# A decoder block on one core: GpSimd's subtractions moved behind VectorE's one-hots, expert weights issued ahead of row stores

## The chip, the cores and the metric

One core of a Trainium2 chip runs the whole kernel as one program. The metric is the time of one execution in microseconds on the device. Before the change three runs gave 703.48, 704.46 and 705.16 us, a median of 704.46.

## What is computed

One decoder block over 512 tokens of width 1024, in float32. Two branches (a chunkwise mLSTM and a differential attention) are merged by sigmoid gates and projected; then comes a routed feed-forward layer with 32 experts. The part that the change touches, cut from the reference:

```python
x = x + gate1 * (merged @ w_out[l])
h2 = rmsnorm(x, norm2_w[l]) * (1.0 + scale2) + shift2
x = x + gate2 * hierarchical_moe(h2, ...)

# hierarchical_moe
pg_top, g_idx = lax.top_k(softmax(hf @ w_rg + b_rg), 1)       # one of 4 groups
pe_top, j_idx = lax.top_k(softmax(e_sel), 2)                  # two of its 8 experts
weights = pg_top * pe_top / jnp.sum(pe_top, axis=-1, keepdims=True)
for e in range(32):
    act = jax.nn.silu(hf @ w_gate[e]) * (hf @ w_up[e])
    y = y + combine[:, e:e + 1] * (act @ w_down[e])
```

## The kernel before, in words

The kernel is written with an order of its own: each engine runs its instructions in the order of the program text, and waits only for data, for buffers and for its queue. The 512 tokens are four tiles of 128 rows, t = 0 to 3.

*The output projection.* `out_proj` multiplies the merged branches with `w_out` in 16 half steps. The first twelve serve all four tiles; the last four are done tile by tile (`x1_of(t)`), so that the rows of one tile are ready while TensorE works on the next. `x1_add` adds the residual on VectorE, in two halves of 512 columns, into the buffer `x1u[t]`. That buffer then holds the block's rows after the first residual.

*Routing of a tile.* `route_a(t)` (L1230) first issues the store of the rows to `out` on SyncE's queue, and then transposes them on TensorE. `route_s` takes the mean square on ScalarE and the power on GpSimd. `route_h` writes the high half of the normalized rows as float16 (`xnh`) on ScalarE. The low half `xnl` is what float16 leaves over. For tiles 0 and 1 VectorE computes it in one step (`route_l`); for tiles 2 and 3 `route_lg` (L1283) lets ScalarE scale `x1u[t]` in place and GpSimd subtract the high half, in two instructions of 512 columns each. `route_b` is the logits. `choices(a)` finds group and experts for the tiles a and a + 1, in some twenty small VectorE steps, each of which is a `yield`, so that other VectorE work can be put between them; for tiles 0 and 1 the two halves of `x1_add(3, ..)` stand after steps 0 and 4. `ranks(a)` counts with matmuls the place of each token at its expert.

*Gather.* `places_of(i, ts)` builds on VectorE the one-hots that send a token's row to its slot at the experts of pair i, two instructions for a pair and two tiles. `gather_mm` multiplies `xnh` and then `xnl` with these, so that the columns of 128 slots come out as a sum. For the first two pairs this is done in two parts, tiles 0 and 1 (`lo2`) and tiles 2 and 3 (`hi2`), so that the first can go on while the choices of the second are made. `idle` puts matmuls without use between them (the counts are `W1`). `evac` writes the gathered columns to `he`, four on ScalarE, four on VectorE. Between them stands `weights` (L1404): two small subtractions on GpSimd, two exponentials on ScalarE, four small VectorE steps.

*Experts.* 16 pairs of experts follow, each with a gate, an up and a down product, and an indirect DMA from GpSimd that adds the result's rows to `out`. That is why the rows have to be stored before.

*Weights.* Each expert has three matrices of 1 MB, 96 loads in all, in the order of use, all issued on SyncE's queue. `refill(n)` issues the next n of the list. The first 20 have buffers of their own: one in the room that the dense part leaves, 15 among the large units that also hold `w_out`, the merged branches (`mgh`, `mgl`) and `xnh`/`xnl`, two in the buffers of the split halves that the projection reads, two in a pool that opens behind the gather. After that a load takes the buffer of a matrix that has been used (`refill_used`). `REF` says how many are issued after which half step of the projection (12 in all), `RT[0]` how many before the tile-by-tile part, and `refill(R0 + R1)` in `out_proj` how many after the last tile's logits are prepared; the rest of the 20 follow in `experts`. SyncE works in program order, too: a load that waits for a buffer holds up the store behind it, and a store that waits for its rows holds up the loads.

*Around the change, in the order of the text:* `x1_of(3)`, `choices(0)` with the two additions of tile 3, `route_h(2)`, `route_a(3)`, `route_s(3)`, `route_b(2)`, `refill(3)`, `route_lg(2)`, `route_h(3)`, `route_lg(3)`; then `route_b(3, first_places)`, which puts `ranks(0)` and the one-hots of tiles 0 and 1 between its matmuls, `choices(2)`, GpSimd's products of one-hots (L1434), the first gathers, `ranks(2)`, the one-hots of tiles 2 and 3 with `weights` between them, and the second gather.

Of the kernel before, what the change touches and what calls it, by code (L numbers as in the profile page):

```python
# [15 lines left out]
AF = mybir.ActivationFunctionType  # L16
# [14 lines left out]
XS = 1024.0  # L31
NU = 18
BR = 5
R0, R1 = 3, 0
RT = (0, 0, 0, 0, 0)
REF = {4: 5, 7: 3, 11: 4}
W0 = (4, 3, 0, 2, 2, 1, 9)
EY, SY = 2, 0
W1 = (3, 2, 2)
GF = False  # L40
LP = lambda n: n % 2
GA = 2
# [15 lines left out]
def block_kernel(ctx, tc, x, c, positions, w_ada, b_ada, norm1_w, w_in, b_igate, b_fgate, conv_w, conv_b,  # L58
# [3 lines left out]
    PE, V, S, G, SP = nc.tensor, nc.vector, nc.scalar, nc.gpsimd, nc.sync  # L62
# [15 lines left out]
    def W2(name, shape, dt=F32):  # L78
        return wk.tile(shape, dt, name=name, tag="w2", bufs=7)
# [4 lines left out]
    def acc(name="acc"):  # L84
        return ps.tile([128, 512], F32, name=name, tag="acc", bufs=4)

    def pt(name="pt", shape=(128, 512), dt=F32):
        return ps.tile(list(shape), dt, name=name, tag="t", bufs=2)

    def ps2(name="ps2"):  # L90
        return ps.tile([128, 2, 512], F32, name=name, tag="s", bufs=1)
# [30 lines left out]
    def load_unit(us, c0, i, n=1024, src=None):  # L122
        kk = 2048 // n
        t = U("wp", [128, kk, n])
        src = win if src is None else src
        SP.dma_start(t, src[i * kk * 128:(i + 1) * kk * 128, c0:c0 + n].rearrange("(k p) f -> p k f", p=128))
        us.append(t)
# [931 lines left out]
    x1u = []  # L1059

    def load_x():

        st["y0"] = st["xw"].tile([128, 1024], F32, name="y0")
        for t in range(4):
            x1u.append(W5("xr", [128, 1024]) if t else st["y0"])
            SP.dma_start(x1u[t], x2[t * 128:(t + 1) * 128])
# [52 lines left out]
    def refill(n, q=SP):  # L1119
        for _ in range(n):  # L1120
            if loads:
                loads.popleft()(q)

    def expert_loads():
        ring.clear()
        loads.clear()
        n = 0
        for i in range(16):
            for w, src, j in (("g", wg_, 8), ("u", wu_, 8), ("d", wd_, 2)):
                for e in (eA[i], eB[i]):  # L1130
                    ld(n, (w, e), src[e], j)
                    n += 1

    ssq2 = const.tile([128, 4, 4], F32, name="ssq2")
# [6 lines left out]
    def nxt(n):  # L1141
        if len(sps) <= n < 16:

            w = wo[n // 4][:, (n // 2) % 2, (n % 2) * 512:(n % 2) * 512 + 512]
            V.tensor_mul(w, w, gbc[0][:, 0, (n % 2) * 512:(n % 2) * 512 + 512])
            sps.append(split(w))
# [4 lines left out]
    def out_proj():  # L1151
        dc.release()
        st["xw"] = ctx.enter_context(tc.tile_pool(name="morew", bufs=1, side="right"))
        routing_tiles()
        expert_loads()
        a_, b_, c_ = pt("oa"), pt("ob"), ps2("oc")
        banks = [a_, b_, c_[:, 0], c_[:, 1]] + [acc("od") for _ in range(4)]

        def mm(t, hh, k, wh, wl):
            ah, al = mgh[k // 4][:, k % 4], mgl[k // 4][:, k % 4]  # L1160
            sl = slice(t * 128, (t + 1) * 128)
            q = banks[2 * t + hh]
            PE.matmul(q, ah[:, sl], wh, start=(k == 0), stop=False)
            PE.matmul(q, ah[:, sl], wl, start=False, stop=False)
            PE.matmul(q, al[:, sl], wh, start=False, stop=(k == 7))

        for n in range(12):
            if n < 2:
                load_unit(wo, 0, n + 2, src=wout)
            if n == 2:  # L1170
                load_x()
            nxt(n + LA)
            for t in range(4):
                mm(t, n % 2, n // 2, *sps[n])
            refill(REF.get(n, 0))
            yield
        nxt(15)
        refill(RT[0])

        def x1_of(t):  # L1180
            for n in (12, 14, 13, 15):
                mm(t, n % 2, n // 2, *sps[n])

        def x1_add(t, *hs):
            for hh in hs or range(2):
                xa = x1u[t][:, hh * 512:(hh + 1) * 512]
                V.tensor_add(xa, banks[2 * t + hh], xa)

        x1_of(0)
        x1_add(0)  # L1190
        refill(RT[1])
        yield
        x1_of(1)
        x1_add(1)
        route_a(0)
        route_s(0)
        refill(RT[2])
        yield
        x1_of(2)
        x1_add(2)  # L1200
        route_a(1)
        route_s(1)
        route_h(0)
        route_b(0)
        refill(RT[3])
        yield

        route_a(2)
        route_l(0)
        route_h(1)  # L1210
        route_b(1)
        route_l(1)
        route_s(2)
        x1_of(3)
        routing_temps()
        for n, _ in enumerate(choices(0)):
            if n in (0, 4):
                x1_add(3, n // 4)
        route_h(2)
        route_a(3)  # L1220
        route_s(3)
        route_b(2)
        refill(R0 + R1)
        route_lg(2)
        route_h(3)
        route_lg(3)

    x1T = {}

    def route_a(t):  # L1230
        xa = x1u[t]
        SP.dma_start(ob[t // 2][:, t % 2], xa)
        h = x1T[t] = [W2("x1T", [128, 512]) for _ in range(2)]
        for hh in range(2):
            p = pt("x2p")
            for j in range(4):
                PE.transpose(p[:, j * 128:(j + 1) * 128], xa[:, (hh * 4 + j) * 128:(hh * 4 + j + 1) * 128], ident)
            if hh and t < 3:
                V.tensor_copy(h[hh], p)
            else:  # L1240
                S.activation(h[hh], p, AF.Copy)

    def route_s(t):
        xa = x1u[t]
        junk = W2("junk", [128, 1024], BF)
        S.activation(junk, xa, AF.Square, accum_out=ssq2[:, t, 0:1])
        G.tensor_scalar(ssq2[:, t, 1:2], ssq2[:, t, 0:1], 1.0 / 1024 / XS ** 2, EPS / XS ** 2, op0=ALU.mult, op1=ALU.add)
        rpow(ssq2[:, t, 2:3], ssq2[:, t, 1:2])

    def route_b(t, between=None):  # L1250
        h = x1T[t]
        p = acc("lgp") if t > 1 else ps2("lgp")[:, 0]
        for j in range(8):
            if j == 4 and between:
                between()
            PE.matmul(p[:, 0:36], h[j // 4][:, (j % 4) * 128:(j % 4 + 1) * 128], wr[:, j], start=(j == 0), stop=(j == 7))
        V.scalar_tensor_tensor(lg[:, t], p[:, 0:36], ssq2[:, t, 2:3], st["rbias"], op0=ALU.mult, op1=ALU.add)
# [8 lines left out]
    def route_h(t):  # L1266
        if t % 2 == 0:
            xn = U("xn", [128, 2, 2, 1024], F16)
            xnh.append(xn[:, 0])
            xnl.append(xn[:, 1])  # L1270
        S.activation(parts_of(t, xnh), rows_of(t), AF.Copy, scale=ssq2[:, t, 2:3])
# [7 lines left out]
    R = {}  # L1279
    flat = lambda ap: ap.rearrange("p t g j -> p t (g j)")  # L1280


    def route_lg(t):  # L1283
        S.activation(x1u[t], x1u[t], AF.Copy, scale=ssq2[:, t, 2:3])
        for a in range(2):
            G.tensor_sub(parts_of(t, xnl)[:, a], rows_of(t)[:, a], parts_of(t, xnh)[:, a])

    def routing_tiles():
        rp = ctx.enter_context(tc.tile_pool(name="routes", bufs=1, side="right"))
        for n, shape, dt in (("m12", [2, 4], F32), ("maskb", [4, 32], BF), ("pos", [4, 32], F32)):  # L1290
            R[n] = rp.tile([128] + shape, dt, name="r" + n)
        R["gm"], R["m1"], R["m2"] = ssq2[:, :, 3], R["m12"][:, 0], R["m12"][:, 1]

        wrf = wr.rearrange("p k f -> p (k f)")
        for c_ in range(2):
            R[f"ohf{c_}"] = wrf[:, c_ * 64:64 + c_ * 64].bitcast(BF).rearrange("p (t g j) -> p t g j", t=4, g=4)
# [55 lines left out]
    def dense():  # L1352
# [9 lines left out]
    oh = {0: W2("oh", [128, 4, 128], F16),  # L1362
          1: st["y0"][:, 512:768].bitcast(F16).rearrange("p (t f) -> p t f", t=4)}
# [3 lines left out]
    def places_of(i, ts=slice(0, 4)):  # L1367
        n = ts.stop - ts.start
        for h, e in enumerate((eA[i], eB[i])):
            V.tensor_tensor(oh[i if st.get("first") else 2][:, ts, h * 64:h * 64 + 64], sio2[:, h, None].to_broadcast([128, n, 64]),  # L1370
                            pos[:, ts, e:e + 1].to_broadcast([128, n, 64]), op=ALU.is_equal)
# [53 lines left out]
    def first_places():  # L1425
        ranks(0)
        places_of(0, lo2)
        places_of(1, lo2)

    route_b(3, first_places)  # L1430
    for _ in choices(2):
        pass
    for c_ in range(2):
        G.tensor_mul(ohf[c_], R["goh"][:, :, :, None].to_broadcast([128, 4, 4, 8]),  # L1434
                     R[f"oh{c_ + 1}"][:, :, None, :].to_broadcast([128, 4, 4, 8]))
    idle(W1[0], qq[1])
    gather_mm(0, pp, range(2), range(2), last=False)
    gather_mm(1, qq, range(2), range(2), last=False)
    wm = acc("warm")
    idle(W1[1], wm)  # L1440
    ranks(2)
    idle(W1[2], wm)
    places_of(0, hi2)
# [184 lines left out]
```

## Time and profile before

| | |
|---|---|
| timed runs | 703.48, 704.46, 705.16 us; median 704.46 |
| profiled execution | 705.96 us, span 704.2 us, mean granted TensorE clock 0.988 |
| TensorE matmul | 674.9 us busy, 96% of the span |
| TensorE weight load | 498.1 us, 71%, beside the matmuls |
| VectorE | 378.1 us, 54% |
| ScalarE | 234.3 us, 33% |
| GpSimd | 202.1 us, 29% |
| transfers | 171.50 MB, mean 244 GB/s; SyncE's queue 165.41 MB |

The profile is one execution; its spans and waits are times from the span's first instruction. The profiled execution's own time is 705.96 us, 1.8 us more than its span; a sum over rows is made against this execution, and the median of the timed runs is 1.50 us below it. A busy TensorE is one with a matmul in work, at whichever of its two clocks (1.2 or 2.4 GHz); the granted clock is 1.00 at the higher.

### The profile page before, as it was taken

To read this page: it belongs to the slowest core of one execution; us is meant where nothing else is said; L and a number is where in the kernel's file an instruction comes from. 1 tells how busy PE (TensorE), PEld (TensorE's weight loads), DVE (VectorE), ACT (ScalarE), POOL (GpSimd) and SP (SyncE) were. 2 spreads that over 40 slices of the span, in tenths; PEclk is the share of its full clock that TensorE was granted. 3 is DMA by queue.
4 is the path that set the end of the run, shared out by engine and by line. 5 is a ranking of instruction groups with operands and counts; after the bars stand their busy time and mean duration, and the time that the engine had idled before them with its cause. 6 is when DMAs were issued, how large, how long until landed. Compare 5 with 4: busy or idle time off the path is not lost. (4 is left out here: it accounts for less than half of the span.)

```text
span 704.2 us, 11486 instructions
## 1 busy us (share of the span) xinstructions
PE 674.9 (96%) x4478; PEld 498.1 (71%) x4478; DVE 378.1 (54%) x769; ACT 234.3 (33%) x513; POOL 202.1 (29%) x211
## 2 busy tenths in 40 slices
PE   6999999999998999999999999899999999999992
PEld 4678877878777777778886888676666666676650
DVE  3556669766685467773597764844322333223311
ACT  4446771452343355544322224441111111111100
POOL 5213253436552122333335431431111112111110
PEclk9999999999999999999999999999999999999998
DMA  9975069215125011045655894798999999999991
GB/s 307 354 228 199 1 257 406 100 55 179 52 75 180 1 60 61 1 180 181 252 180 190 337 423 186 283 403 326 382 382 375 407 397 389 386 373 382 408 380 24
DMA packets 47402, 171.50 MB, mean 244 GB/s; under 512 B 8025, under 2 KB 16354, under 8 KB 33006
## 3 DMA queue, kind: packets, MB, share of 16 engines
q1 hardware_dynamic: 44526, 165.41, 61.1%
q0 software_dynamic: 2752, 5.28, 3.8%
q8 instruction: 37, 0.61, 0.3%
q14 instruction: 23, 0.19, 0.1%
q10 hardware_dynamic: 64, 0.02, 0.0%
HBM read 164.37 MB, written 10.51 MB: 248 GB/s over the span
## 5 line engine op out<-in xcount | busy, mean ns | idle before, releaser
L443 POOL TENSOR_TENSOR hl<-wp,hl 128x512 fp32r<-128x512 f32 x60 | 84.8, 1415 | 172.8 <-ACT hl L442 157.3
L442 ACT ACTIVATE hl<-wp 128x512 fp32r<-128x512 f32 x120 | 74.5, 628 | 102.1 <-PE acc L500 44.9
L1559 PE MATMUL gu<-we,he 128*64 128x256 f32 x784 | 92.6, 379 | 0.0
L499 PE MATMUL acc<-hTh,hl 128*128 128x512 f32 x220 | 90.7, 412 | 0.1
L501 PE MATMUL acc<-hTh,hl 128*128 128x512 f32 x220 | 87.5, 398 | 0.0
L500 PE MATMUL acc<-hTl,hl 128*128 128x512 f32 x220 | 86.9, 395 | 0.0
L1559 PEld LDWEIGHTS gu<-we,he 128*64 128x64 f32 x784 | 59.7, 137 | 32.5 <-issue 6.8
L443 DVE TENSOR_TENSOR hl<-wp,hl 128x512 fp32r<-128x512 f32 x60 | 52.7, 879 | 51.5 <-ACT hl L442 51.4
L1383 PEld LDWEIGHTS <-xn 128*128 128x128 f16 x1024 | 61.6, 115 | 7.2 <-issue 5.4
L1563 ACT ACTIVATE sg<-gu 128x256 f32<-128x256 f32 x16 | 6.2, 385 | 170.7 <-PE gu L1559 170.7
L1383 PE MATMUL gp<-oh,xn 128*128 128x128 f16 x960 | 61.1, 224 | 0.5 <-DVE oh L1370 0.4
L1591 POOL DMA_INDIRECT out<-y,wr x11 | 19.3, 1756 | 140.2 <-DVE y L1586 116.2
L1564 DVE TENSOR_TENSOR sg<-sg,gu 128x256 f32<-128x256 f32 x16 | 6.8, 423 | 92.7 <-ACT sg L1563 92.7
L503 PE MATMUL acc<-hl,hTh 128*128 128x512 f32 x128 | 52.6, 411 | 0.0
L499 PEld LDWEIGHTS acc<-hTh,hl 128*128 128x128 f32 x220 | 41.8, 190 | 14.7 <-issue 4.7
L505 PE MATMUL acc<-hl,hTl 128*128 128x512 f32 x128 | 50.2, 392 | 0.0
L504 PE MATMUL acc<-hl,hTh 128*128 128x512 f32 x128 | 50.0, 391 | 0.0
L501 PEld LDWEIGHTS acc<-hTh,hl 128*128 128x128 f32 x220 | 41.6, 189 | 10.2
L1584 PE MATMUL o<-we,sg 128*64 128x512 f32 x192 | 47.4, 598 | 1.1 <-issue 1.1
L500 PEld LDWEIGHTS acc<-hTl,hl 128*128 128x128 f32 x220 | 41.9, 190 | 8.6
L868 DVE SCALAR_TENSOR_TENSOR wada<-wada,ccols 128x1024 f32<-128x1024 f32 x28 | 41.5, 1506 | 1.9 <-DMA wada<-in_w_ada 1.9
L1401 DVE TENSOR_SCALAR he<-gp,AB 128x128 f32<-128x128 f32 x64 | 21.9, 404 | 23.3 <-PE gp L1383 20.8
(364 smaller groups left out, 1174.5 us busy)
## 6 DMA issues: line engine op xcount, KB each, us to landing
we<-in_w_gate SPq DMA_DIRECT2D x25, 1024.0 KB
we<-in_w_up SPq DMA_DIRECT2D x24, 1024.0 KB
we<-in_w_down SPq DMA_DIRECT2D x24, 1024.0 KB
wp<-in_w_in SPq DMA_DIRECT2D x20, 1024.0 KB
wada<-in_w_ada SPq DMA_DIRECT2D x16, 1024.0 KB
ada<-in_w_ada SPq DMA_DIRECT2D x16, 512.0 KB
wx<-in_w_gate SPq DMA_DIRECT2D x6, 1024.0 KB
wp<-in_w_out SPq DMA_DIRECT2D x4, 1024.0 KB
```

The lines of the kernel that those rows point to most:

```text
L442: S.activation(hi, src, AF.Copy)
L443: (G if LP(n) else V).tensor_sub(lo, src, hi.bitcast(F32))
L499: PE.matmul(g.banks[b], wh[:, sl], ah, start=st, stop=False)
L500: PE.matmul(g.banks[b], wh[:, sl], al, start=False, stop=False)
L501: PE.matmul(g.banks[b], wl[:, sl], ah, start=False, stop=en)
L503: PE.matmul(g.banks[b], ah[:, sl], wh, start=st, stop=False)
L504: PE.matmul(g.banks[b], ah[:, sl], wl, start=False, stop=False)
L505: PE.matmul(g.banks[b], al[:, sl], wh, start=False, stop=en)
L868: V.scalar_tensor_tensor(t0[:, sl], cur[:, sl], ccol[:, j:j + 1], t0[:, sl], op0=ALU.mult, op1=ALU.add)
L1383: PE.matmul(ps_[c_][:, jj * 128:(jj + 1) * 128], parts_of(t, part)[:, c_, :, jj], o[:, t], start=first and part is xnh and jj == 0 and t = ...
L1559: PE.matmul(gu[r, k * 256:(k + 1) * 256], h[:, j, r], wt[key, e][:, j], start=(j == 0), stop=(j == 7), skip_group_check=True)
L1584: PE.matmul(o[r], aT[:, j, r], wt["d", e][:, j, n * 512:(n + 1) * 512], start=(j == 0), stop=(j == 1), skip_group_check=True)
```

## The change

Four things are changed. The scaling of tiles 2 and 3 by ScalarE stays where it was, in a function of its own (`route_ls`), while GpSimd's subtractions (`route_lg`) are issued in `first_places`, behind a copy of one element out of the last of VectorE's first one-hots, so that GpSimd starts them only when these are done. `refill` stands before `route_a(3)`, and so before the last tile's store, instead of behind `route_b(2)`, and issues four loads instead of three; two more loads are issued before the tile-by-tile part, ahead of all four stores. The second half of tile 3's addition follows step 2 of the choices instead of step 4. The unused matmuls between the gathers are 2, 4 and 2 instead of 3, 2 and 2.

```diff
-R0, R1 = 3, 0
-RT = (0, 0, 0, 0, 0)
+R0, R1 = 4, 0
+RT = (2, 0, 0, 0, 0)
-W1 = (3, 2, 2)
+W1 = (2, 4, 2)
         for n, _ in enumerate(choices(0)):
-            if n in (0, 4):
-                x1_add(3, n // 4)
+            if n in (0, 2):
+                x1_add(3, n // 2)
         route_h(2)
+        refill(R0 + R1)
         route_a(3)
         route_s(3)
         route_b(2)
-        refill(R0 + R1)
-        route_lg(2)
+        route_ls(2)
         route_h(3)
-        route_lg(3)
+        route_ls(3)

+    def route_ls(t):
+        S.activation(x1u[t], x1u[t], AF.Copy, scale=ssq2[:, t, 2:3])
+
     def route_lg(t):
-        S.activation(x1u[t], x1u[t], AF.Copy, scale=ssq2[:, t, 2:3])
         for a in range(2):
             G.tensor_sub(parts_of(t, xnl)[:, a], rows_of(t)[:, a], parts_of(t, xnh)[:, a])

     def first_places():
         ranks(0)
         places_of(0, lo2)
         places_of(1, lo2)
+
+        G.tensor_copy(R["ix"][0:1, 2:3], oh[1][0:1, 1, 127:128])
+        for t in (2, 3):
+            route_lg(t)
```

## Rows read from the trace of the kernel before

**Rows 1.** The page's part 1: busy us, share of the span, instructions.

```profile
PE 674.9 (96%) x4478; PEld 498.1 (71%) x4478; DVE 378.1 (54%) x769; ACT 234.3 (33%) x513; POOL 202.1 (29%) x211
```

**Rows 2.** Waits of PE, 425 to 704: total us, times, longest.

```profile
PE rkp L1348 <- DVE rmaskb L1338: 2.1, 1, 2.1
...
PE o L1584 <- issue: 1.1, 2, 0.6
...
PE gu L1559 <- ACT he L1399: 0.4, 1, 0.4
```

**Rows 3.** The same view of SyncE's queue, 380 to 704.

```profile
SPq L1112 <- PE gu L1559: 90.5, 30, 12.4
```

**Rows 4.** Timeline, 447 to 463: start, us, engine, line, operation, tiles, count.

```profile
447.81 4.63 POOL L1286 TENSOR_TENSOR xn<-xr,xn 128x512 f16<-128x512 f32 x4 [0.20 <-ACT xr L1284]
448.17 2.09 DVE L1370 TENSOR_TENSOR oh<-sio,rpos 128x128 f16<-128x128 bf16 x2
450.18 2.40 DVE L1370 TENSOR_TENSOR y<-sio,rpos 128x128 f16<-128x128 bf16 x2
452.51 0.24 DVE L1257 SCALAR_TENSOR_TENSOR lg<-lgp,ssq,rbias 128x36 f32<-128x36 f32 x1
452.77 1.95 PE L1383 MATMUL gp<-y,xn 128*128 128x128 f16 x32
457.86 0.49 DVE L1370 TENSOR_TENSOR oh<-sio,rpos 128x128 f16<-128x128 bf16 x2
458.40 3.47 PE L1383 MATMUL gp<-oh,xn 128*128 128x128 f16 x32 [0.40 <-DVE oh L1370]
461.91 1.51 ACT L1399 ACTIVATE he<-gp,AB 128x128 f32<-128x128 f32 x4 [4.17 <-PE gp L1383]
462.42 0.43 PE L1559 MATMUL gu<-wx,he 128*64 128x256 f32 x1 [0.44 <-ACT he L1399]
```

**Rows 5.** Windows near the end: us, engines' busy us, PEclk, DMA share, GB/s.

```profile
680.00:684.00 4.00, 4.00 (x40) 3.23 (x38) 0.75 (x1) 0.00 (x0) 1.54 (x1) 1.00 1.01 417
684.00:688.00 4.00, 3.07 (x30) 2.10 (x26) 0.42 (x1) 0.39 (x1) 0.00 (x0) 1.00 0.61 179
```

**Rows 6.** Timeline of ScalarE and GpSimd in the same stretch.

```profile
448.82 1.15 ACT L1284 ACTIVATE xr<-xr,ssq 128x1024 f32<-128x1024 f32 x1
456.75 0.41 POOL L1434 TENSOR_TENSOR wr<-rtmp 128x128 bf16<-128x128 f32 x1 [0.84 <-DVE rtmp L1319]
457.11 0.22 POOL L1406 TENSOR_TENSOR rtmp<-lg,ssq 128x16 f32<-128x16 f32 x1
457.53 0.21 ACT L1409 ACTIVATE rtmp<-rtmp 128x4 f32<-128x4 f32 x1
```

**Rows 7.** Timeline: SyncE's queue, its waiters, and the end of tile 3's projection.

```profile
378.50 0.38 SPq L126 DMA_DIRECT2D wp<-in_w_out  x1
379.34 0.34 SPq L900 DMA_DIRECT2D n<-in_norm_w  x1
384.61 0.26 POOL L901 TENSOR_SCALAR n<-n 128x8 f32<-128x8 f32 x1 [5.04 <-DMA n<-in_norm_w]
429.63 0.34 SPq L1232 DMA_DIRECT2D out<-y  x1
432.98 11.70 SPq L1232 DMA_DIRECT2D out<-xr  x3
442.96 0.40 PE L1165 MATMUL od<-hl,mgl 128*128 128x512 f32 x1
```

**Rows 8.** Windows around a store alone, and with loads queued.

```profile
430.00:432.00 2.00, 2.00 (x13) 1.66 (x12) 0.34 (x1) 0.00 (x0) 0.00 (x0) 1.00 0.66 262
447.00:460.00 13.00, 10.43 (x112) 8.51 (x112) 10.94 (x39) 3.31 (x5) 7.05 (x11) 0.81 0.99 406
```

**Rows 9.** Windows at TensorE's gap and behind it.

```profile
455.00:457.00 2.00, 0.19 (x3) 0.12 (x2) 1.69 (x10) 0.00 (x0) 0.66 (x2) 1.00 1.01 426
458.50:461.50 3.00, 3.00 (x31) 3.00 (x31) 0.92 (x5) 0.00 (x0) 2.00 (x6) 0.51 1.02 426
```

## The prediction, made before the changed kernel was run

> **What bounds the kernel now.** I read the engines' shares first, then TensorE's list of waits, then the timeline around the last stretch in which TensorE waits for anything, then SyncE's queue and the windows beside it. TensorE is busy for 96% of the span [rows 1]. From 425 us on it waits 2.1 us for the mask of the last two token tiles and 0.4 us for the first gathered columns, and for no weight transfer at all [rows 2]. SyncE, which issues the weights, is the one that waits, 90.5 us in 30 pieces, for TensorE to give buffers back [rows 3]. So from the first expert matmul at 462.42 [rows 4] to the end TensorE sets the pace. The transfers are only just in time: they are still running after 684 [rows 5], when the last pair's up projection has just begun, and the ring of buffers ties them to TensorE, so that if TensorE starts later or earlier they shift with it. The question is therefore what the change does to 462.42 and to the speed from there.
>
> What sets 462.42 is a chain [rows 4]: VectorE's logits of tile 3 at 452.51, its choices and ranks, the one-hots at 457.86, TensorE's gather of tiles 2 and 3 at 458.40, ScalarE's eviction at 461.91, the first expert matmul. In front of it stand four one-hots in 2.09 + 2.40 us beside GpSimd's four subtractions of 4.63 us; the same two one-hots at 457.86, with GpSimd out of the way, take 0.49.
>
> **The change part by part.**
>
> *GpSimd behind the one-hots.* Four one-hots at 0.49 us a pair are 0.98 instead of 4.49, so tile 3's logits come 3.4 us earlier at best, about 449.1. From logits to hi-tile one-hots it was 457.86 - 452.51 = 5.35. If the moved subtractions left the choices alone, the one-hots would start at 454.5. The four held-up one-hots took about one subtraction each (4.49 / 4 = 1.12 against 4.63 / 4 = 1.16), so as the other bound four of the choices' operations wait one subtraction each: 454.5 + 4 x 1.16 = 459.1, worse than before. Either way VectorE is not what is late next, as the following step shows. The small copy that holds GpSimd back is not in the trace; by the small GpSimd operations [rows 6] it is 0.2 to 0.4 us, if nothing hides it; here GpSimd has to wait for longer anyway (next step), so I count 0.
>
> The Trainium skill, "SBUF — State Buffer", section "Who interferes with whom", says that a VectorE instruction with two SBUF inputs is shut out by a GpSimd instruction that reads SBUF. By that rule the second bound above is the right one, and the gain on VectorE mostly moves from the one-hots to the choices; without the rule it would be 3.4 us. The rows on the one-hots [rows 4] fit it; no row of before has the long subtractions beside the choices. The sum would be the same by either, since the store decides it; by the rule, rival A would come out at its slow end, without it at its fast one.
>
> *The last store behind four loads.* This is the step that decides. The scaling of tile 3's rows by ScalarE is done in place, in the buffer that the store to `out` reads, so it can't start before that store has landed. Before, the store was issued at 444.3 (last of the three in the row from 432.98, which ends at 444.68) into an idle queue and the scaling started at 448.82 right behind ScalarE's own work [rows 6, 7]. Now `refill(4)` stands in front of it on the same queue. These loads take the buffers that tile 3's output projection has read last, so they can't go before 442.96 + 0.40 = 443.4 [rows 7]; the queue is idle then. How a transfer fares behind a load is in [rows 7]: the 4 KB of `n` were issued at 379.34, after a 1 MB load issued at 378.50, and GpSimd, waiting for them, began at 384.61, 5.3 us after their issue. So the queue is served in order. A store alone keeps the transfer engines busy for 0.66 x 2.0 = 1.3 us, and they begin 0.4 us or more after its issue at 429.63; four loads are 4.19 MB, at 406 GB/s 10.3 us [rows 8]. Sum: 443.4 + 0.7 + 10.3 + 1.3 + some 1.0 for a cold start and the landing = 456.7; I take 457, between 455.7 (nothing for start and landing) and 458 (twice that). Before, it was there before 448.8.
>
> From there the order of the engines' queues gives the first expert matmul, step by step [rows 4, 6]: scaling 1.14; two subtractions of tile 3, 2 x 1.16 = 2.3; behind them on GpSimd the two products of one-hots, 2 x 0.41 = 0.8; the two small subtractions and the exponentials on ScalarE, 457.11 to 457.74, 0.6; then ScalarE's eviction to the first matmul, 462.42 - 461.91 = 0.5 (the evictions are queued on ScalarE behind the exponentials, and these behind the scaling). Together 5.3, with six hand-overs of some 0.05 us 5.6: 457 + 5.6 = 462.6, against 462.42. TensorE's gather of the low halves needs the same subtractions and is done about 0.3 us before that. So the wait for the store takes back all that the one-hots gave: +0.2 us, between -1.1 and +1.2 with the bounds of the landing.
>
> *The clock.* What TensorE does in that time is little: it has gathered tiles 0 and 1 by about 454.5, fills in a few warm-up matmuls (W1 adds one in sum: 0.2 us, hidden in the same wait), gathers the high halves of tiles 2 and 3 in about 1 us and then stands until 462.6 but for some 1 us of low halves. Before, it had one such gap, nearly idle from 455.0 to 457.0, and the granted clock then fell to half (1.2 GHz): 0.51 from 458.5 to 461.5, so that the 32 gathers took 3.47 us, where 32 of them took 1.95 at full clock [rows 4, 9]. That low stretch lay on the gather. In the new order it falls on the first expert matmuls, which are limited by TensorE alone: each us at half clock loses half a us. A stretch like the one of before costs 3.47 - 1.95 = 1.5 us; with its edges 1.5 to 1.7, and a second one in a row is possible. The bounds are 0 and 3.2; I take 1.6.
>
> *Two loads ahead of all stores.* `RT[0] = 2` puts 2.10 MB, 5.2 us, ahead of the store issued at 429.63, for which the queue was empty [rows 7, 8]; the first store is later by at most these 5.2 us, the second and third by less, and nobody waits for them before ScalarE's scaling of tile 2, just ahead of that of tile 3 at 448.82. Cost 0. Their gain is that the weights run 5 us ahead; as TensorE waits for no weights [rows 2], this is worth 0 at the end. Without this cover it would be bounded by the same 5 us.
>
> *Row 3's second addition two steps sooner.* VectorE's steps are 0.2 us apart, so the last row is ready 0.2 us earlier, and its store behind the loads doesn't notice: 0, at best -0.2.
>
> Sum: +0.2 + 1.6 = +1.8 us. On the profiled execution, 705.96 us for a span of 704.2, this is 707.8. That execution was 1.5 us over the median of the timed runs, so the forecast for the median is 704.46 + 1.8 = 706.3.
>
> **The rivals.**
>
> *A: the store isn't late* (the loads wait for something longer, are overtaken, or ScalarE doesn't have to wait). Then the hi-tile one-hots set the time, at 454.5 to 459.1 by the two bounds above. The gather starts 0.5 later and takes 1.95 at full clock, since the gap is short, and 0.9 lie between its end and the first expert matmul (the gather's last result to the eviction, and 461.91 to 462.42): 457.9 to 462.4. It can't come before TensorE has done its first gathers and the four warm-ups either: 452.77 + 1.95 = 454.7 before, two more warm-ups 0.6, the ranks and one-hots 0.5 each [rows 4], and the same 1.95 + 0.9 give 459.2. So -3.2 to 0 us; I take the middle of the one-hots, 456.8, which gives 460.2: -2.2, 702.3. The landing decides: this holds when the store has landed by about 454, since 454 + 5.6 is 459.6. For it: two of the loads have a different kind of buffer (the split halves). Against it: the row of `n`, and 10 us of transfers that nothing shortens.
>
> *B: late, but the clock does not fall on the experts,* or the landing is at the low end: -1.1 to +1.2, I take +0.3: 704.8. For it: before, the low stretch was over when the gather was, and TensorE has some gathers in its gaps here, too. Against it: from about 458 to 462.6 it has 1 us of work, even less than in the gap of before.
>
> *C: more:* two low stretches in a row, or a landing at 458 with a whole one: +3.2 to +4.5, 708.3 on average.
>
> That the additional prefetch shortens the end is excluded by [rows 2, 3]: buffers come back only as TensorE uses them.
>
> **How the numbers follow.** About 0.2% (1.4 us) is what a measurement of this kernel tells from no change. Forecast 0.45 (705.4 to 707.4), B 0.26, A 0.17, C 0.12. Faster by over 0.2%: A less its upper edge, 0.15, and a little of B, 0.16. Within: the rest of A and B and the forecast's lower edge, 0.29. Slower: the rest, 0.55. The range from 702.2 to 708.9 leaves out about 0.08 below (half of A) and 0.06 above; as cases of both signs are in it, the forecast's own range is 705.4 to 707.4.
>
> **What would show it.** In the changed profile: the first four one-hots in about 1 us and tile 3's logits near 449.2; SyncE's last store issued at about 445.5, after four loads; ScalarE's scaling of tile 3 waiting for a transfer, and starting at 456 to 458; GpSimd's products of one-hots after 460; the first expert matmul at 462 to 463.5; granted clock 0.5 in a stretch after it. It is wrong if ScalarE's scaling starts before 453, or if TensorE's first expert matmul comes before 461 at full clock; and wrong in another way if TensorE later waits for weights.

## The result, and the profile after

The changed kernel takes 708.40 us, median of 6 runs (707.15 to 710.07); the kernel before took 704.42 beside it, median of 6 (703.34 to 705.35). The ratio is 1.0051, 95% interval 1.0032 to 1.0069: slower by half a per cent. The profiled execution is the slowest of the six, 710.07 us for a span of 708.4 (before: 705.96 and 704.2), so its span has grown by 4.1 us.

The timeline of the changed kernel around the gathers (start, us, engine, line, operation, tiles, count), answering [rows 4, 6]:

```profile
448.15 0.49 DVE L1372 TENSOR_TENSOR oh<-sio,rpos 128x128 f16<-128x128 bf16 x2
448.56 0.49 DVE L1372 TENSOR_TENSOR y<-sio,rpos 128x128 f16<-128x128 bf16 x2
...
449.33 2.25 POOL L1288 TENSOR_TENSOR xn<-xr,xn 128x512 f16<-128x512 f32 x2
...
449.63 0.26 DVE L1257 SCALAR_TENSOR_TENSOR lg<-lgp,ssq,rbias 128x36 f32<-128x36 f32 x1 [0.58 <-PE lgp L1256]
...
450.12 0.37 DVE L1315 TENSOR_TENSOR rtmp<-lg,ssq 128x8 f32<-128x8 f32 x1
...
450.53 1.09 DVE L1317 TENSOR_TENSOR rtmp<-rtmp,io 128x8 f32<-128x8 f32 x1
452.07 0.16 DVE L1319 TENSOR_REDUCE rtmp<-rtmp 128x2 f32<-128x8 f32 x1 [0.46 <-DVE rtmp L1317]
...
456.60 0.22 DVE L1352 SCALAR_TENSOR_TENSOR rpos<-rkp,rmaskb 128x64 f32<-128x64 f32 x1 [0.85 <-PE rkp L1350]
...
456.86 0.49 DVE L1372 TENSOR_TENSOR oh<-sio,rpos 128x128 f16<-128x128 bf16 x2
457.41 1.11 PE L1385 MATMUL gp<-oh,xn 128*128 128x128 f16 x17 [0.40 <-DVE oh L1372]
...
457.95 1.15 ACT L1284 ACTIVATE xr<-xr,ssq 128x1024 f32<-128x1024 f32 x1 [9.57 <-DMA out<-xr]
459.18 2.25 POOL L1288 TENSOR_TENSOR xn<-xr,xn 128x512 f16<-128x512 f32 x2 [7.60 <-ACT xr L1284]
...
460.38 2.04 PE L1385 MATMUL gp<-oh,xn 128*128 128x128 f16 x15 [1.87 <-POOL xn L1288]
461.40 0.77 POOL L1440 TENSOR_TENSOR wr<-rtmp 128x128 bf16<-128x128 f32 x2
...
462.12 0.22 POOL L1408 TENSOR_TENSOR rtmp<-lg,ssq 128x16 f32<-128x16 f32 x1
...
462.65 1.49 ACT L1401 ACTIVATE he<-gp,AB 128x128 f32<-128x128 f32 x4
...
463.15 0.69 PE L1565 MATMUL gu<-wx,he 128*64 128x256 f32 x1 [0.61 <-ACT he L1401]
```

VectorE's first four one-hots take 0.9 us instead of 4.5, and the hi-tile one-hots come 1.0 us earlier than in [rows 4]. But ScalarE's scaling of tile 3 waits 9.57 us until the store `out<-xr` has landed, and everything from 457.95 to the first expert matmul is the chain behind it. That matmul takes 0.69 us instead of 0.43: it runs at half clock, as the windows below show.

SyncE's queue, answering [rows 7]: four loads, and the last store behind them.

```profile
442.98 0.83 SPq L1112 DMA_DIRECT2D we<-in_w_up  x2
443.90 1.06 SPq L1112 DMA_DIRECT2D ws<-in_w_down  x2
445.08 0.39 SPq L1232 DMA_DIRECT2D out<-xr  x1
```

The trace's landing records put the loads at 447.9, 450.9, 453.4 and 456.7 and the store at 457.87, 12.8 us after its issue; the store before it, in an empty queue, was there 2.6 us after its issue (435.87 to 438.5). TensorE's waits from 425 us on (total, times, longest), answering [rows 2]:

```profile
PE gp L1385 <- POOL xn L1288: 1.9, 1, 1.9
...
PE gu L1565 <- ACT he L1401: 0.6, 1, 0.6
PE gu L1565 <- DMA wx<-in_w_up: 0.5, 1, 0.5
```

The first is new, and so is the last, a wait for weights in the last pair. Windows of the changed kernel (us, busy us of the engines, PEclk, DMA share, GB/s), answering [rows 5, 9]:

```profile
457.00:460.00 3.00, 1.11 (x18) 0.95 (x16) 0.35 (x2) 1.15 (x1) 0.82 (x1) 1.00 0.02 8
460.50:467.00 6.50, 5.82 (x37) 3.78 (x38) 4.03 (x16) 4.22 (x12) 5.06 (x12) 0.50 0.68 256
684.00:688.00 4.00, 3.52 (x32) 2.38 (x30) 0.00 (x0) 0.00 (x0) 1.46 (x1) 1.00 1.01 384
688.00:692.00 4.00, 3.07 (x28) 1.82 (x24) 0.42 (x1) 0.38 (x1) 0.00 (x0) 1.00 0.30 81
```

TensorE does 1.1 us of work in 3, then the granted clock is at its lower level (0.50, 1.2 GHz) for 6.5 us, most of it on experts. At the end the transfers run on until after 688.

One table carries most of what follows. All is counted from the end of the last matmul of tile 3's projection (443.36 in the kernel before, 442.79 + 0.40 in the changed one). That point is not the same in two profiles, even of kernels with the same code up to there: 442.57 in one run below and 445.63 in another. The first four columns are starts behind it; the fifth is from the first to the second pair's first matmul, the sixth from the last pair's first matmul to the end of its last product.

| kernel | scaling, tile 3 | logits, tile 3 | hi one-hots | first expert | pair 1 | last pair | timed ratio |
|---|---|---|---|---|---|---|---|
| before | 5.46 | 9.15 | 14.50 | 19.06 | 16.66 | 12.77 | 1 |
| changed | 14.77 | 6.45 | 13.67 | 19.96 | 18.63 | 14.33 | 1.0051 |
| e1 store first | 5.24 | 6.08 | 14.54 | 19.18 | 16.65 | 12.77 | 1.0000 |
| e2 own buffer | 5.11 | 6.44 | 14.53 | 17.62 | 16.64 | 13.11 | 1.0000 |
| e3 loads only | 14.51 | 7.22 | 12.39 | 19.70 | 19.42 | 12.77 | 1.0053 |
| e4 subtractions only | 5.24 | 6.44 | 14.54 | 17.58 | 16.65 | 13.76 | 1.0000 |
| e5 TensorE kept busy | 14.96 | 6.44 | 14.06 | 20.15 | 16.65 | 13.98 | 1.0029 |
| e6 store from ScalarE | 10.94 | 6.39 | 14.09 | 17.54 | 16.65 | 12.77 | 1.0009 |
| e7 low half on VectorE | - | 7.00 | 14.09 | 17.18 | 16.65 | 12.76 | 0.9989 |
| e8 the same, loads as before | - | 7.01 | 13.87 | 16.96 | 16.65 | 14.24 | 0.9987 |
| e9 e7 without filling | - | 7.01 | 12.34 | 15.43 | 16.65 | 12.75 | 0.9974 |
| e10 e9, filling earlier | - | 7.15 | 12.48 | 15.57 | 16.65 | 12.77 | 0.9975 |
| e11 e8 without filling | - | 7.00 | 12.35 | 15.44 | 16.65 | 12.76 | 0.9959 |

So the 4.1 us are: +0.90 to the first expert matmul, +1.97 in the first pair, +1.56 in the last, less some 0.15 before the projection's end and as much behind the last product.

### The profile page after: what moved, and what is told of

It reads as the page before. It is cut to its first block, busy times and chain, and to the rows that moved or that the text cites. A ratio compares the mean times of both kernels' runs of the same rounds, so it can differ in the third digit from the quotient of the medians.

```text
span 708.4 us, 11491 instructions
## 1 busy us (share of the span) xinstructions
PE 678.1 (96%) x4479; PEld 499.7 (71%) x4479; DVE 376.4 (53%) x769; ACT 234.0 (33%) x513; POOL 202.1 (29%) x212
## 3 DMA queue, kind: packets, MB, share of 16 engines
q0 software_dynamic: 2752, 5.28, 3.8%
## 5 line engine op out<-in xcount | busy, mean ns | idle before, releaser
L1565 PE MATMUL gu<-we,he 128*64 128x256 f32 x784 | 94.5, 382 | 0.0
```

The lines of the kernel that those rows point to most:

```text
L1565: PE.matmul(gu[r, k * 256:(k + 1) * 256], h[:, j, r], wt[key, e][:, j], start=(j == 0), stop=(j == 7), skip_group_check=True)
```

## The experiments

Theory: the store behind four loads makes the scaling late, and the lull that follows puts half clock on the experts. Rivals: the moved subtractions do the harm, by holding up the choices; or the weights' order does.

**The store alone, two ways.** e1 puts the loads behind the store again; e2 leaves the order and writes tile 3's scaled rows into tile 1's buffer, so that ScalarE need not wait.

```diff
-        refill(R0 + R1)
         route_a(3)
+        refill(R0 + R1)
```

> The changed kernel with one line moved: the four loads are issued behind the last tile's store instead of ahead of it; all else is as changed. Theory (the late store): ScalarE's scaling of tile 3 starts at about 448.4 with no wait, GpSimd ends its four subtractions at about 454, the first expert matmul comes at 459.5 to 462.4 instead of 463.15, with no half-clock stretch on the experts, and the time is 702.0 to 704.8 us where the kernel before has 704.4. Rival (the moved subtractions and the new counts of warm-up matmuls cost the time, the late store only coincides): the time stays at 707 to 709.

```diff
-        S.activation(x1u[t], x1u[t], AF.Copy, scale=ssq2[:, t, 2:3])
+        S.activation(x1u[1 if t == 3 else t], x1u[t], AF.Copy, scale=ssq2[:, t, 2:3])
...
-            G.tensor_sub(parts_of(t, xnl)[:, a], rows_of(t)[:, a], parts_of(t, xnh)[:, a])
+            G.tensor_sub(parts_of(t, xnl)[:, a], rows_of(1 if t == 3 else t)[:, a], parts_of(t, xnh)[:, a])
```

> The changed kernel, loads still ahead of the last store, but tile 3's scaled rows go into the buffer of tile 1, whose store has long landed, so that nobody waits for the last store. Theory (the wait for the store): as with the store first, 702.0 to 704.8 us, though the store itself lands at 457.9 as in the changed kernel. Rival (the four loads themselves cost the time, by what they take from the transfers or by late weights): 707 to 709, as changed.

Measured: 704.92 us, ratio 1.0000 [0.9986, 1.0014], and 704.63, 1.0000 [0.9984, 1.0015]. Either way the loss is gone, and no gain is left (e1's time is 0.1 us above the range expected, with before at 705.08 beside it). The timeline of e1:

```profile
443.09 0.33 SPq L1232 DMA_DIRECT2D out<-xr  x1
...
443.51 1.21 SPq L1112 DMA_DIRECT2D we<-in_w_up  x2
...
447.57 1.15 ACT L1284 ACTIVATE xr<-xr,ssq 128x1024 f32<-128x1024 f32 x1
...
448.45 4.50 POOL L1288 TENSOR_TENSOR xn<-xr,xn 128x512 f16<-128x512 f32 x4
...
456.87 0.49 DVE L1372 TENSOR_TENSOR oh<-sio,rpos 128x128 f16<-128x128 bf16 x2
...
457.42 3.55 PE L1385 MATMUL gp<-oh,xn 128*128 128x128 f16 x32 [0.40 <-DVE oh L1372]
```

The scaling doesn't wait, and all four subtractions now lie beside the choices: the one-hots at 456.87 are 14.54 behind the projection, as before (14.50). The gather takes 3.55 us, again at half clock, as in [rows 4].

**Each half of the change alone.** e3 is the kernel before with the loads moved; e4 is the changed kernel with the loads as before.

```diff
-R0, R1 = 3, 0
-RT = (0, 0, 0, 0, 0)
+R0, R1 = 4, 0
+RT = (2, 0, 0, 0, 0)
...
+        refill(R0 + R1)
         route_a(3)
         route_s(3)
         route_b(2)
-        refill(R0 + R1)
```

> The kernel before with the loads' part of the change alone: two ahead of the stores, four ahead of the last store; GpSimd's subtractions, the warm-up matmuls and the additions as before. Theory: ScalarE waits for the last store until about 458, the first expert matmul comes at 463 to 464 with a half-clock stretch behind it, 707 to 709 us: the whole loss comes with this part. Rival (the loss needs the moved subtractions): 703.5 to 705.5, as before.

e4 is the same diff the other way, on the changed kernel.

> The changed kernel with the loads as before (three, behind the last store, none ahead of the others): the moved subtractions, the new warm-up counts and the earlier addition alone. Theory: no wait for a store; the choices of tiles 2 and 3 are held up by the four subtractions instead of the one-hots, so the hi-tile one-hots come at 456.5 to 458.5 (457.86 before) and the time is 702.5 to 705.0 us. Rival (the moved subtractions lose): 706.5 or more. If the clear gain that the one-hots promise by themselves (3.4 us) were kept: under 702.

Measured: e3 709.02 us, 1.0053 [1.0032, 1.0074], the whole loss; e4 705.15, 1.0000 [0.9985, 1.0016], no loss, 0.15 us above its expected range. In e3 ScalarE's waits from 440 to 470 have the store as in the changed kernel:

```profile
ACT xr L1284 <- DMA out<-xr: 9.1, 1, 9.1
```

There VectorE is even 2.1 us ahead at the hi one-hots (12.39 against 14.50), since two of the subtractions wait for the scaling too and leave it alone; it is of no use. A window of e3 over the first experts:

```profile
462.30:469.00 6.70, 5.74 (x33) 3.27 (x32) 5.67 (x20) 4.22 (x12) 4.97 (x14) 0.50 0.84 315
```

The granted clock is 0.50, and pair 1 lasts 2.76 us longer. VectorE's timeline in e4 has what the moved subtractions cost:

```profile
451.13 0.37 DVE L1315 TENSOR_TENSOR rtmp<-lg,ssq 128x8 f32<-128x8 f32 x1
451.54 1.08 DVE L1317 TENSOR_TENSOR rtmp<-rtmp,io 128x8 f32<-128x8 f32 x1
453.08 0.16 DVE L1319 TENSOR_REDUCE rtmp<-rtmp 128x2 f32<-128x8 f32 x1 [0.46 <-DVE rtmp L1317]
453.27 0.47 DVE L1321 TENSOR_TENSOR rtmp<-io,rtmp 128x8 f32<-128x8 f32 x1
453.78 1.14 DVE L1330 TENSOR_TENSOR rtmp<-lg,rtmp 128x64 f32<-128x64 f32 x1
```

With no subtraction beside them, operations of these lines on tiles of 8 or 16 columns take 0.17 us (further on in e4), and the one on 64 columns 0.22 (in the first choices). The excess is 0.20 + 0.91 + 0.46 + 0.30 + 0.92 = 2.8 us, and the logits had come 9.15 - 6.44 = 2.7 us earlier. The two cancel: 14.54 against 14.50.

**The clock.** e5 is the changed kernel with unused matmuls in the lull, 12 ahead of the second gather instead of 2 and four behind it.

```diff
-W1 = (2, 4, 2)
+W1 = (2, 4, 12)
...
     gather_mm(0, pp, range(2), range(2, 4), first=False)
+    idle(4, wm)
```

> The changed kernel with matmuls without use in the time in which TensorE waits for the late low halves: 12 instead of 2 ahead of the gather of tiles 2 and 3, and four behind it. The first expert matmul should come at about 463.1 as in the changed kernel. Theory (the clock is the second term of the loss): no half-clock stretch on the experts, the second pair begins at about 479.8 instead of 481.8, and the time is some 2 us under the changed kernel's: 705.5 to 707.5. Rival (the first pair is slow for another reason, late weights or its own evictions): second pair at 481 or later, 707.5 to 709.

Measured: 707.16 us, 1.0029 [1.0017, 1.0042], 1.2 us below the changed kernel's 708.40 (which was timed beside other runs of before; by the ratios, 0.0022 x 705 = 1.6). The two intervals overlap, so the times by themselves leave the gain unsure; the windows show what changed:

```profile
457.00:461.00 4.00, 4.00 (x36) 2.31 (x35) 0.72 (x3) 1.15 (x1) 0.77 (x1) 1.00 0.18 71
461.00:467.00 6.00, 5.33 (x56) 3.55 (x55) 3.01 (x13) 3.55 (x11) 4.64 (x12) 1.00 0.61 206
```

The clock stays at its higher level and pair 1 takes 16.65 instead of 18.63, though the store is as late as ever. So the late start and the slow first pair are two costs, one from the store and one from the lull: TensorE's little work between 457 and 460.

**Another queue.** e6 issues tile 3's store from ScalarE.

```diff
-        SP.dma_start(ob[t // 2][:, t % 2], xa)
+        (S if t == 3 else SP).dma_start(ob[t // 2][:, t % 2], xa)
```

> The changed kernel with the last tile's store issued on ScalarE's queue instead of SyncE's, where the four loads stand ahead of it. Theory (it is the order within one queue that delays the store): it lands by about 450, ScalarE's scaling of tile 3 starts by 450.5, and the time is as with the store first, 703.5 to 706 us. Rival (the transfer engines are full and serve in order of issue whatever the queue): it lands near 457 and the time stays at 707 to 709.

Measured: 705.30 us, 1.0009 [0.9997, 1.0021]; most of the loss is gone, and nothing is gained. Timeline of ScalarE:

```profile
442.51 0.38 ACTq L1232 DMA_DIRECT2D out<-xr  x1
...
452.69 1.16 ACT L1284 ACTIVATE xr<-xr,ssq 128x1024 f32<-128x1024 f32 x1 [5.48 <-DMA out<-xr]
```

The store is issued 0.8 us behind the projection instead of 1.9, but it still takes 10.1 us beside them (it lands at 452.61, between the second load at 450.64 and the third at 454.31). So the landing came out as neither case expected: not by 450 and not near 457. It is early enough here, as the scaling is then no longer last. The profiled execution (702.77) is this kernel's fastest of 12, so its columns in the table flatter it.

**A version that gains.** The two halves of the change point to one thing: tile 3's subtraction should be beside nothing and wait for nothing. In e7 VectorE makes tile 3's low half itself (`route_l`, scaling and subtraction in one, out of the unscaled rows), behind the hi one-hots; GpSimd does tile 2 alone, and no later than before. e8 is the same with the loads as before.

```diff
         route_ls(2)
+        route_lg(2)
         route_h(3)
-        route_ls(3)
...
-        G.tensor_copy(R["ix"][0:1, 2:3], oh[1][0:1, 1, 127:128])
-        for t in (2, 3):
-            route_lg(t)
...
     places_of(0, hi2)
+    route_l(3)
     weights()
```

> The changed kernel with the low halves divided: GpSimd subtracts tile 2 at once, as before the change, and VectorE makes tile 3's low half in one step behind the hi-tile one-hots (as tiles 0 and 1 have it), so that no engine waits for the last store and GpSimd is never beside the choices. Expected from what was seen: two of the four first one-hots held up (lg of tile 3 near 451), hi-tile one-hots near 456.5, 1.5 us of VectorE behind them, first expert matmul at 459.8 to 461.0, 702.0 to 704.0 us. Against it: weights that come too late at the end (705), or the half-clock stretch on the gather or the experts (704 to 706).

> The same with the loads as before the change (three, behind the last store). If the weights that run ahead are worth nothing, as the prediction had it: the same time as with them, within 0.7 us. If they are worth something once TensorE is earlier: 1 to 2 us slower, with a wait for weights in the last pairs.

Measured: 703.63 us, 0.9989 [0.9976, 1.0003], and 704.28, 0.9987 [0.9976, 0.9999]: both a little below before, by less than 0.2%, and e7's interval still holds 1. VectorE's timeline in e7 says what is last now:

```profile
456.85 0.23 DVE L1352 SCALAR_TENSOR_TENSOR rpos<-rkp,rmaskb 128x64 f32<-128x64 f32 x1 [2.13 <-PE rkp L1350]
```

VectorE waits 2.13 us for TensorE's ranks, which are queued behind the first gathers, most of them at half clock, and four unused matmuls of 1.03 us together. e9 and e11 take the unused matmuls out of e7 and e8, and e10 puts eight of them in front of the logits of tiles 2 and 3 in e9.

```diff
-W1 = (2, 4, 2)
+W1 = (2, 0, 0)
```

> The kernel with tile 3's low half on VectorE (loads and store order as in the change), and the unused matmuls between the first gathers and the second taken out (W1 = (2, 0, 0) instead of (2, 4, 2)). In its parent TensorE ran the first gathers at half clock until 455.1, then four unused matmuls (1.03 us) and only then the ranks of tiles 2 and 3, for which VectorE waited 2.1 us. If this filling is on the path, ranks, one-hots and the first expert matmul come 0.9 to 1.2 us earlier (first expert matmul about 16.1 us behind the last matmul of tile 3's projection, instead of 17.18), and the time is 0.5 to 1.2 us below the parent's 703.63. The rival: without the filling the granted clock falls to half again on the second gather or the first experts, which costs 1.5 to 2 us; then the time is the parent's or up to 1 us above.

> As the run without the filling, and four unused matmuls of 512 columns put in front of the logits of tile 2 and of tile 3 each, where TensorE otherwise has transposes and 36-column products, after which its clock fell to half at 4.5 us behind the projection. If the fall follows from what TensorE does there, the half-clock stretch of 6.8 us starts later or is gone, the first gathers take 4 us instead of 6, and the first expert matmul comes up to 1.5 us earlier than without the early filling; time 701.5 to 703. The rival: eight matmuls cost 8 x 0.22 = 1.8 us in front of tile 3's logits and move ranks and one-hots back by as much, with the clock falling all the same: 0.5 to 1.8 us slower than without.

> As the run without the filling, with the loads as in the kernel before (no two ahead, three behind tile 2's logits). If the weights' stream bounds an earlier start (the last pair waited 1 to 1.5 us for its weights in the two profiles in which the experts began 1.5 to 2.9 us earlier with the loads as before), this one gains nothing over its own parent's 704.28, and the run with the loads ahead is 0.6 to 1.5 us faster. If the prefetch is worth nothing, the two are within 0.4 us.

Measured: e9 702.45 us, 0.9974 [0.9961, 0.9988]; e10 703.41, 0.9975 [0.9959, 0.9991]; e11 702.20, 0.9959 [0.9945, 0.9974]. From e8 to e11 the intervals are apart: the filling was on the path. From e7 to e9 they overlap, and the 1.75 us that the first expert matmul is earlier in e9's profile are more than the four matmuls; the last section comes back to this. In e11:

```profile
457.73 0.23 DVE L1352 SCALAR_TENSOR_TENSOR rpos<-rkp,rmaskb 128x64 f32<-128x64 f32 x1 [0.37 <-PE rkp L1350]
457.99 0.49 DVE L1372 TENSOR_TENSOR oh<-sio,rpos 128x128 f16<-128x128 bf16 x2
```

The wait is 0.37 us and the first expert matmul comes 15.4 us behind the projection, 3.6 earlier than before, with pair 1 at full clock. e10's profile shows no stretch at half clock around the gathers at all, yet it gains nothing over e9 (703.41 us is 0.4 above its expected range): the gathers are then faster than VectorE's choices, which TensorE waits for (1.2 us for `rmaskb`). And the loads ahead gain nothing either: e9 and e11 agree within their intervals, so the case that the prefetch would be worth 0.6 to 1.5 us in this pair fell. e11 is 0.4% faster than the kernel before and 0.9% faster than the changed one. Most of the 0.4% came with taking out the filling (0.9987 to 0.9959); that was not tried on the kernel before, so how much of it needs the low half on VectorE is not shown.

## Why the prediction was right or wrong, point by point

It said slower, by the right mechanism, and 706.3 us; 708.4 is inside the range of 702.2 to 708.9 but above the likeliest case's own 705.4 to 707.4. By its time what came is rival C (708.3, chance 0.12): a landing near its late end and a long stretch at half clock. By its terms it is so only in part: in the profile they make 0.90 + 1.97 = 2.9 us, less than C's 3.2, and the rest is a wait for weights that no case held. That 708.4 lies so near C's 708.3 is in part luck.

*GpSimd behind the one-hots.* Right that VectorE wouldn't be what is late. The hi one-hots came at 456.86, between the two bounds of 454.5 and 459.1: 7.2 us behind the logits instead of 5.35, as only one tile's subtractions met the choices; with all four (e4) it is 8.1, an excess of 2.8 us where the second bound had 4.6. The Trainium skill, "SBUF — State Buffer", "Who interferes with whom", says that a VectorE instruction with two SBUF inputs contends with a GpSimd instruction that reads SBUF, and the runs bear it out: 1.08 us for one that takes 0.17 alone, while a reduction with one input kept its 0.16.

*The last store behind four loads.* Confirmed: e3 has the whole loss without the moved subtractions, e1 and e2 lose nothing with them. The landing was 457.87 for 457 forecast, and the chain from there 5.28 us for 5.6. The term came to +0.7 in absolute times, +0.9 from the projection's end, for +0.2: inside its bounds, the landing mis-sized by 0.9. The "some 1.0 for a cold start and the landing" rests on no row of before. The changed profile shows that the loads were the long part: the first landed 4.9 us after its issue and the others 3.0, 2.5 and 3.3 us after one another, 13.7 us from first issue to last landing, and the store 1.2 us later.

*The clock.* Confirmed by e5, and mis-sized: the low stretch lasted from 460.5 to 467 and beyond its ends a little, twice that of [rows 9], and took 1.97 us from pair 1 for 1.6 forecast (2.76 in e3). "A second one in a row is possible" was held for rival C, not the sum. A longer stretch is what came.

*Two loads ahead, and the second addition.* Both at 0, and right as far as runs go: e1 holds both and times as before; neither was run by itself.

*Weights.* Here the prediction failed: "as TensorE waits for no weights [rows 2], this is worth 0 at the end" took for granted that it would stay so, and the sum has no term for a wait, though a later wait for weights is among its own signs of being wrong. The margin was small already before: there the last down matrix landed at 688.08, 0.97 us ahead of the first product of its kind in that pair (689.05). In the changed kernel's profiled execution the last pair lost 1.56 us, the up matrix landing at 687.13 and the last down matrix at 693.29, when the down products were ready to start at 692.84. That the change causes it is not shown: e4, e5 and e8 lost 1.0 to 1.5 us there, with loads ahead and without, while e3, e6, e7, e9 and e10 with them, and before, e1 and e11, lost nothing (e2 0.3).

The landing records show what is late. A load has sixteen of them, and of the last down matrix the sixteenth came 3.9 to 4.4 us behind the thirteenth in the four profiles that lost 1 us or more (changed: 689.12 and 693.29), and 1.2 to 2.6 us in the nine others (before: 686.46 and 688.08). So most of the matrix was there in time, and a few of its parts trailed. Why they trail in some executions, and how often, is left open. As e3 times like the changed kernel without this loss in its profile, the first two terms (2.9 us in one profile, 3.4 in the other) are the ones to rely on; the rest of the 4.0 between the medians is not settled.

*Rivals A and B.* A's condition, that ScalarE doesn't wait for the store, did not come about in the change but was made in e1 and e2: they gave 0 and not the -2.2 forecast, since the choices had paid for the one-hots, the slow end of A's range. B failed on the clock; e5 made its condition, a late store without the low stretch, and measured +2.0 by its ratio where B had +0.3, as the first expert matmul came 1.1 us later than before and its last pair lost 1.2 us.

## What to carry to other kernels

Before a load is moved ahead of a store in one queue, look for who reuses the store's source: here nobody read the stored rows, but an in-place scaling waited for the landing, 12.8 us behind 4 MB. An engine moved out of another's way runs into what comes next, so count the operations it will lie beside; 2.7 us gained on four one-hots came back as 2.8 on five small steps (e4). And unused matmuls that keep the clock up are work in TensorE's queue: they pay in a lull that must be waited out, and cost as soon as something behind them is wanted.

## What the runs showed of the hardware

A store of 0.5 MB issued from another engine's queue got only a little ahead of the loads: issued just behind the third of four loads of 1 MB, it landed between the second and the third, 10.1 us after its issue (e6), against 12.8 behind all four in their own queue and 2.6 alone. A VectorE operation of 8 columns beside GpSimd's 512-column subtractions took 1.09 us instead of 0.17, and the reduction after it began 0.46 us after its end instead of 0.03.

And where the half-clock stretch falls can differ between profiles of kernels that run the same up to there. e7 and e9 differ only behind the first gathers, yet these 64 matmuls span 5.8 us in e7 and 4.6 in e9:

```profile
449.97 3.62 PE L1385 MATMUL gp<-oh,xn 128*128 128x128 f16 x32
453.38 2.40 PE L1385 MATMUL gp<-y,xn 128*128 128x128 f16 x32
```

```profile
449.14 2.85 PE L1385 MATMUL gp<-oh,xn 128*128 128x128 f16 x32 [0.27 <-DVE oh L1372]
...
451.82 1.95 PE L1385 MATMUL gp<-y,xn 128*128 128x128 f16 x32
```

The granted clock is 0.50 from 447.5 to 454.3 in e7, and only to 451.0 in e9. Likewise the second gather is at half clock in e1's profile (3.55 us, first expert at 19.18) and at full clock in e4's (1.95 us, 17.58), while the two time alike; these also differ in the place of the loads. A gain of some 1.5 us in one profile can be that and no more.
